# A diffusion backbone layer on one core: the down projection as seven quarter products instead of eight

## The chip, the cores and the metric

The kernel runs on one core of a Trainium2 chip. The metric is the device time of one execution in microseconds (us). The engines are named as in the profile: PE (matrix products; PEld are its weight loads), DVE (vector), ACT (scalar, activations), POOL, and SP, whose queue issues most of the DMAs. Lower is better.

## The reference, cut to what matters

One layer: a token mixer (spatial gating and gated linear attention, with a context prefix), then a channel mixer with a 3x3 depthwise convolution over the token grid, and a final norm. There are 512 tokens of 1024 channels and a hidden width of 2816, all in 32-bit floats. The change is in the second half of the channel mixer and in what follows it:

```python
def _conv_ffn(h, rows, w_up, conv_w, conv_b, w_down):
    a, val = _split(h @ w_up, (D_FF, D_FF))                  # 512 x 1024 @ 1024 x 5632
    ...                                                      # a: 3x3 depthwise convolution + bias
    return (gelu(a) * val) @ w_down                          # 512 x 2816 @ 2816 x 1024

x = x + g2x * _conv_ffn(hx2, ...)
return _rms_norm(x, final_norm_g)
```

## The kernel before, in words

Every large product is made of three products of fp32r operands: each 32-bit operand is split into a high half, which is a rounded copy, and a low half, which is the operand minus its high half, and high x high, high x low and low x high are accumulated in one PSUM bank. Splitting a tile is therefore one cast and one subtraction. For weights the cast is on ACT and the subtraction on DVE (`stream_split`, L186 and L187); for activations both are on DVE unless an engine is named (`split_act`, L273 and L274).

Weights come through one list, `specs`, in the order of their use, 512 KB an entry, loaded by SP's queue into four `raw` buffers (L174) and split into five `wh` and five `wl` buffers. `weights()` hands out the next entry and asks for the splits of two entries and the loads of three more.

The order of the instructions on each engine is set at compile time by a list scheduler: what stands earlier in the program has priority, and an instruction that is ready in its model may overtake one that isn't. Tiles come from pools of fixed size: `heap` (44 buffers of 2 KB a partition), `late` (27), and the PSUM pools `mm` and `gl` (four banks each). `in_order` adds edges that keep a group of instructions of an engine in program order.

In the up projection, 22 hidden tiles `f` of 128 channels are made. Each takes two products of 24 matmuls (L281), one for `a` and one for `val`, with the 512 tokens as columns. `conv_part` then copies `a` out of PSUM (ACT, L1183), starts the accumulator `cacc` with the middle tap (ACT, L1185), adds eight taps on DVE (L1191), applies Gelu (ACT, L1192) and multiplies by `val` (DVE, L1193). The 22 results stay in `heap` as `gact`, hidden channels on the partitions and tokens along the free side.

The down projection (from L1211 on) runs over two halves of the 1024 output columns, `hf`. A half has four PSUM banks, one for each tile of 128 tokens, and runs over the 22 hidden tiles; `down` (L1220 to L1225) issues the three matmuls of 512 columns. The first half also splits `gact` into `gs` (L273, L274); the second uses the same splits again. The last six hidden tiles, `TAIL`, are done token tile by token tile, so that the output of one tile can be finished while the next one is multiplied; the very last one is cut into 384 and 128 columns. `out_add` multiplies a bank by `g2` (L1232) and adds it to the residual `x1` (L1233), `out_step` also sums the squares (ACT, L1238), and `out_tok` makes the norm's factor (L1249 to L1251: DVE, ACT with Sqrt, DVE), scales both halves of the token tile (ACT L1253, DVE L1255) and stores them.

Of the kernel before, what the change touches and what calls it, by code (L numbers as in the profile page):

```python
# [33 lines left out]
def backbone_kernel(  # L34
# [212 lines left out]
    for d in range(2):  # L247
        raw = late([96, 512], s="w2r")
# [21 lines left out]
    def split_act(src, n=512, s="a", lo_pool=heap, hi_pool=heap, eng=None):  # L270
        hi = hi_pool([P, n], F32R, s=s + "h")
        lo = lo_pool([P, n], F32R, s=s + "l")
        (eng or V.tensor_copy)(hi, src)  # L273
        V.tensor_tensor(lo, src, hi.bitcast(F32), op=ALU.subtract)  # L274
        return hi, lo
# [311 lines left out]
    for k in range(KT):  # L587
        g = max(i for i in range(NG) if G0[i] <= k)
# [9 lines left out]
        n = 0  # L598
# [43 lines left out]
    for d in range(2):  # L642
        t_ = late([P, 4, P], s="pmask")
# [422 lines left out]
    for j in range(KT):  # L1066
        w = weights()
        ps = mm()
# [25 lines left out]
    for j in range(KT):  # L1094
        w = weights()
        ps = mm()
# [4 lines left out]
        w = weights()  # L1101
        ps = mm()
# [26 lines left out]
    for i in range(2):  # L1129
        ps = gl()  # L1130
# [44 lines left out]
    wide_tm(mg, wo_done, lambda: None)  # L1175


    gact = []

    def conv_part(f, pa, pv):  # L1180
        wcol = lambda tap: ccol[:, tap * FT + f:tap * FT + f + 1]
        a_ = heap([P, 8, GW], s="ca")
        A.copy(a_, pa)  # L1183
        acc = heap([P, 8, GW], s="cacc")
        A.activation(acc, pa, AF.Identity, bias=ccol[:, 198 + f:199 + f], scale=wcol(4))  # L1185
        for tap in (0, 1, 2, 3, 5, 6, 7, 8):
            dy, dx = tap // 3 - 1, tap % 3 - 1
            r0, r1 = max(0, -dy), 8 - max(0, dy)
            c0, c1 = max(0, -dx), GW - max(0, dx)
            o = acc[:, r0:r1, c0:c1]  # L1190
            V.scalar_tensor_tensor(o, a_[:, r0 + dy:r1 + dy, c0 + dx:c1 + dx], wcol(tap), o, op0=ALU.mult, op1=ALU.add)  # L1191
        A.activation(acc, acc, AF.Gelu)  # L1192
        V.tensor_tensor(acc, acc, pv.rearrange("p (r w) -> p r w", w=GW), op=ALU.mult)  # L1193
# [8 lines left out]
    conv_part(1, pss[2], pss[3])  # L1202
    for f in range(2, FT):
# [8 lines left out]
    for hf in range(2):  # L1212
        t_ = late([P, 512], s="fng")
        dma(t_, final_norm_g[hf * 512:(hf + 1) * 512].unsqueeze(0).to_broadcast([P, 512]))
        fng.append(t_)
    gs = []
    ss3 = const([P, 4, 3], "ss3")
    xg = []

    def down(ps, g, w, kk, t, c0, n, first, last):  # L1220
        gh, gl_ = g
        wh, wl = w
        for i, (a, b) in enumerate(((gh, wh), (gh, wl), (gl_, wh))):
            T.matmul(ps, a[:, t * P:(t + 1) * P], b[:, kk, c0:c0 + n], start=(first and i == 0),  # L1224
                     stop=(last and i == 2))  # L1225

    TAIL = 6

    def out_add(pv, hf, t, c0, n):
        tmp = late([P, n], s="yt")  # L1230
        xv = x1[t][hf][:, c0:c0 + n]
        V.tensor_tensor(tmp, pv, bc_g["g2", hf][:, c0:c0 + n], op=ALU.mult)  # L1232
        V.tensor_tensor(xv, xv, tmp, op=ALU.add)  # L1233
# [6 lines left out]
    def out_tok(t, part, before):  # L1240

        b_, r = small(1, "n3b"), small(1, "n3r")
        start = len(traced())
        part()
        if before > 1:
            V.reduce_sum(b_, ss3[:, t, :before], axis=AX.X)
            V.tensor_scalar(b_, b_, 1.0 / D, EPS, op0=ALU.mult, op1=ALU.add)
        else:
            V.tensor_scalar(b_, ss3[:, t, 0:1], 1.0 / D, EPS, op0=ALU.mult, op1=ALU.add)  # L1249
        A.activation(r, ss3[:, t, before:before + 1], AF.Sqrt, bias=b_, scale=1.0 / D)  # L1250
        V.reciprocal(r, r)  # L1251
        in_order(start, V.engine)
        A.mul(xg[t], xg[t], r)  # L1253
        adma(out[0, t * P:(t + 1) * P, 0:512], xg[t])
        V.scalar_tensor_tensor(x1[t][1], x1[t][1], r, fng[1], op0=ALU.mult, op1=ALU.mult)  # L1255
        dma(out[0, t * P:(t + 1) * P, 512:1024], x1[t][1])

    for hf in range(2):
        pss = [(mm if hf else gl)() for _ in range(4)]
        for kc_ in range((FT - TAIL) // 2):  # L1260
            w = weights()
            for kk in range(2):
                k = 2 * kc_ + kk
                if hf == 0:
                    gs.append(split_act(gact[k].rearrange("p r w -> p (r w)"), s="g"))
                for t in range(4):
                    down(pss[t], gs[k], w, kk, t, 0, 512, k == 0, hf == 1 and t == 3 and k == FT - TAIL - 1)
        wl3 = [weights() for _ in range(TAIL // 2)]
        if hf == 0:
            for k in range(FT - TAIL, FT):  # L1270
                gs.append(split_act(gact[k].rearrange("p r w -> p (r w)"), s="g", lo_pool=late))
        else:

            out_add(pss[3], 1, 3, 0, 512)
        for t in range(4):
            pieces = [(0, 384), (384, 128)] if hf and t == 3 else [(0, 512)]
            for i, (c0, n) in enumerate(pieces):
                ps = gl() if hf and t == 3 else pss[t]
                for k in range(FT - TAIL, FT):
                    down(ps[:, :n], gs[k], wl3[(k - FT + TAIL) // 2], k % 2, t, c0, n,  # L1280
                         hf == 1 and t == 3 and k == FT - TAIL, k == FT - 1)
                step = lambda: out_step(ps[:, :n], hf, t, c0, n, hf + i)
                if hf == 0 or i + 1 < len(pieces):
                    step()
                else:
                    out_tok(t, step, hf + i)
            if hf == 0:
                xg.append(late([P, 512], s="xg"))
                V.tensor_tensor(xg[t], x1[t][0], fng[0], op=ALU.mult)


# [28 lines left out]
```

## Time and profile before

| | us |
|---|---|
| median of three runs | 957.38 |
| lowest and highest | 956.77 and 957.75 |
| span of the profiled execution | 956.3 |
| PE busy | 935.2 |
| DVE busy | 654.4 |
| ACT busy | 351.0 |

For the profiled execution the page gives the span, from its first to its last instruction, and no device time of its own; the median lies 1.1 us above the span. The page cuts the span into 40 slices of 23.9 us, with the busy share of each engine in tenths. The up projection of the channel mixer ends at 828.5, the products of the down projection at 949.4. A line such as `L274 DVE TENSOR_TENSOR gl<-cacc,gh 128x512` reads: line of the kernel, engine, operation, tile written and tiles read, partitions x elements, and then the count, the busy time and the mean duration in ns. A line of the timeline begins with the start and the duration in us, and ends with the idle time before it and what ended it.

### The profile page before, as it was taken

To read this page: it belongs to the slowest core of one execution; us is meant where nothing else is said; L and a number is where in the kernel's file an instruction comes from. 1 tells how busy PE (TensorE), PEld (TensorE's weight loads), DVE (VectorE), ACT (ScalarE), POOL (GpSimd) and SP (SyncE) were. 2 spreads that over 40 slices of the span, in tenths; PEclk is the share of its full clock that TensorE was granted. 3 is DMA by queue.
4 is the path that set the end of the run, shared out by engine and by line. 5 is a ranking of instruction groups with operands and counts; after the bars stand their busy time and mean duration, and the time that the engine had idled before them with its cause. 6 is when DMAs were issued, how large, how long until landed. Compare 5 with 4: busy or idle time off the path is not lost.

```text
span 956.3 us, 12491 instructions
## 1 busy us (share of the span) xinstructions
PE 935.2 (98%) x4810; PEld 784.1 (82%) x4810; DVE 654.4 (68%) x1157; ACT 351.0 (37%) x593; POOL 13.4 (1%) x34
## 2 busy tenths in 40 slices
PE   6999999999999999999999999999999999999997
PEld 5677898988888888888878889988888888888886
DVE  5567768688699655597564357887777777893414
ACT  5146445566433222222222135433333333311313
POOL 3000000000000000000000000000000000000000
PEclk9999999999999999999999999999999999999999
DMA  9940412032137563683532443333333333232302
GB/s 274 342 126 24 113 43 61 29 111 67 38 118 220 173 205 85 215 270 104 158 91 88 148 122 111 103 96 88 110 89 105 93 89 110 69 114 84 110 1 88
DMA packets 147144, 111.95 MB, mean 117 GB/s; under 512 B 5849, under 2 KB 123941, under 8 KB 147085
## 3 DMA queue, kind: packets, MB, share of 16 engines
q1 hardware_dynamic: 145005, 109.72, 38.0%
q10 hardware_dynamic: 1728, 1.22, 0.4%
q8 instruction: 38, 0.62, 0.3%
q0 software_dynamic: 352, 0.22, 0.1%
q14 instruction: 21, 0.17, 0.1%
HBM read 109.04 MB, written 2.10 MB: 116 GB/s over the span
## 4 chain that ended last, share of the span: by engine, by line
PE 89%; DVE 5%; DMA 2%; ACT 2%; issue 1%; SPq 0%; ACTq 0%; DVEq 0%
PE mm L281 53%; PE gl L1224 7%; PE mm L1224 6%; PE mm L307 5%; PE gl L741 3%; PE mm L300 3%; PE mm L531 1%; PE mm L292 1%; PE gl L307 1%; PE mm L845 1%; DVE bc L709 1%; PE gl L531 1%; PE gl L772 1%; PE gl L1040 1%; PE gl L455 1%
## 5 line engine op out<-in xcount | busy, mean ns | idle before, releaser
L186 ACT CAST wh<-raw 128x1024 fp32r<-128x1024 f32 x140 | 147.3, 1053 | 368.1 <-PE mm L281 248.3
L187 DVE TENSOR_TENSOR wl<-raw,wh 128x1024 fp32r<-128x1024 f32 x140 | 170.6, 1220 | 126.4 <-ACT wh L186 126.0
L281 PE MATMUL mm<-h2h,wh 128*128 128x512 f32 (+1 forms) x352 | 133.5, 379 | 0.0
L281 PE MATMUL mm<-h2l,wh 128*128 128x512 f32 (+1 forms) x352 | 133.5, 379 | 0.0
L281 PE MATMUL mm<-h2h,wl 128*128 128x512 f32 (+1 forms) x352 | 133.5, 379 | 0.0
L1191 DVE SCALAR_TENSOR_TENSOR cacc<-ca,ccol,cacc 128x441 f32<-128x441 f32 (+2 forms) x176 | 121.8, 695 | 4.6 <-ACT cacc L1185 0.5
L281 PE MATMUL mm<-hxh,wh 128*128 128x512 f32 x296 | 116.5, 393 | 0.0
L281 PE MATMUL mm<-hxh,wl 128*128 128x512 f32 x296 | 115.7, 391 | 0.0
L281 PE MATMUL mm<-hxl,wh 128*128 128x512 f32 x296 | 115.4, 390 | 0.0
L281 PEld LDWEIGHTS mm<-h2h,wh 128*128 128x128 f32 x352 | 66.2, 188 | 12.6
L281 PEld LDWEIGHTS mm<-h2l,wh 128*128 128x128 f32 x352 | 66.2, 188 | 12.4
L281 PEld LDWEIGHTS mm<-h2h,wl 128*128 128x128 f32 x352 | 66.2, 188 | 12.4
L281 PEld LDWEIGHTS mm<-hxh,wl 128*128 128x128 f32 x296 | 55.6, 188 | 11.7 <-issue 0.2
L281 PEld LDWEIGHTS mm<-hxh,wh 128*128 128x128 f32 x296 | 55.6, 188 | 11.6 <-issue 0.5
L281 PEld LDWEIGHTS mm<-hxl,wh 128*128 128x128 f32 x296 | 55.6, 188 | 11.2 <-issue 0.2
L1008 DVE SCALAR_TENSOR_TENSOR acc<-wa,cs,acc 128x512 f32<-128x512 f32 x64 | 45.6, 744 | 4.8 <-DMA wa<-in_w_ada_dram 4.7
L1224 PE MATMUL gl<-wh,gl 128*128 128x512 f32 (+2 forms) x100 | 37.9, 379 | 0.0
L1224 PE MATMUL gl<-wl,gh 128*128 128x512 f32 (+2 forms) x100 | 37.9, 379 | 0.0
L1224 PE MATMUL gl<-wh,gh 128*128 128x512 f32 (+2 forms) x100 | 37.8, 378 | 0.0
L1192 ACT ACTIVATE cacc<-cacc 128x512 f32<-128x512 f32 x22 | 13.9, 632 | 60.5 <-DVE cacc L1191 60.5
L1224 PE MATMUL mm<-wh,gh 128*128 128x512 f32 x82 | 31.9, 389 | 0.0
L1224 PE MATMUL mm<-wl,gh 128*128 128x512 f32 x82 | 31.9, 389 | 0.0
(366 smaller groups left out, 1733.6 us busy)
## 6 DMA issues: line engine op xcount, KB each, us to landing
raw<-in_w_in_dram SPq DMA_DIRECT2D x54, 512.0 KB, 3.9
wa<-in_w_ada_dram SPq DMA_DIRECT2D x96, 256.0 KB, 4.9
raw<-in_ffn_w_up_dram SPq DMA_DIRECT2D x44, 512.0 KB, 3.8
raw<-in_ffn_w_down_dram SPq DMA_DIRECT2D x22, 512.0 KB, 3.6
raw<-in_w_br_a_dram SPq DMA_DIRECT2D x8, 512.0 KB, 4.5
raw<-in_w_br_b_dram SPq DMA_DIRECT2D x8, 512.0 KB, 4.3
raw<-in_w_o_dram SPq DMA_DIRECT2D x8, 512.0 KB, 3.6
xin<-in_x_dram SPq DMA_DIRECT2D x8, 256.0 KB, 3.2
```

The source lines that it names most:

```text
L186: A.copy(wh, raw)
L187: V.tensor_tensor(wl, raw, wh.bitcast(F32), op=ALU.subtract)
L281: T.matmul(ps, a[:, k, :], b[:, c0:c0 + n], start=(k == 0 and i == 0), stop=(k == KT - 1 and i == 2))
L292: T.matmul(ps, a[:, k, :], b[:, c0:c0 + n], start=(k == 0 and i == 0), stop=(k == KT - 1 and i == 2))
L300: T.matmul(ps, a[:, t * P:(t + 1) * P], b[:, k % 4, :], start=(k == 0 and i == 0), stop=(k == KT - 1 and i == 2))
L307: T.matmul(ps, a[:, t * P:(t + 1) * P], b[:, k % 2, :], start=(k == 0 and i == 0), stop=(k == KT - 1 and i == 2))
L531: T.matmul(fps[i], a, b, start=(k == 0 and z == 0), stop=(k == KT - 1 and z == 2))
L741: T.matmul(ps, p_, q_, start=(start and z == 0), stop=(stop and z == 2))
L1008: V.scalar_tensor_tensor(acc[j], w_, cs[:, k, 0:1], acc[j], op0=ALU.mult, op1=ALU.add)
L1191: V.scalar_tensor_tensor(o, a_[:, r0 + dy:r1 + dy, c0 + dx:c1 + dx], wcol(tap), o, op0=ALU.mult, op1=ALU.add)
L1192: A.activation(acc, acc, AF.Gelu)
L1224: T.matmul(ps, a[:, t * P:(t + 1) * P], b[:, kk, c0:c0 + n], start=(first and i == 0), stop=(last and i == 2))
```

## The change

The down projection is `G @ W` with `G` of 512 tokens x 2816 and `W` of 2816 x 1024. Both are cut into quarters: the tokens into two halves of 256, the output columns into two halves of 512, and the hidden tiles into the even ones (`e`, tile 2p of pair p) and the odd ones (`o`, tile 2p+1); there are eleven pairs. With A11, A21 the two token halves of `e`, A12, A22 those of `o`, B11, B12 the two column halves of the even rows of `W`, and B21, B22 those of the odd rows, the change makes (Winograd's form of Strassen's method):

```
S1 = A21 + A22   S2 = S1 - A11   S3 = A11 - A21   S4 = A12 - S2
T1 = B12 - B11   T2 = B22 - T1   T3 = B22 - B12   T4 = T2 - B21
P1 = A11 B11  P2 = A12 B21  P3 = S4 B22  P4 = A22 T4  P5 = S1 T1  P6 = S2 T2  P7 = S3 T3
C11 = P1 + P2       C12 = P1 + P6 + P5 + P3
C21 = P1 + P6 + P7 - P4       C22 = P1 + P6 + P7 + P5
```

Each of the seven products has 256 tokens, 512 columns and 1408 hidden channels. The first pass over the pairs makes P1, P5, P6 and P7 in eight banks. Then DVE and ACT combine them, and the second pass accumulates P2, P3 and P4 (its operand has the other sign) on top of three of the four. The sums over tokens, S1 to S4, are made on DVE in the up projection, after every second hidden tile (`token_sums`, four subtractions and additions of 256 columns). The sums over weights are made in `x_prep` (T1, T2 and T3, in the first pass) and `rb_prep` (T4). In all of them the high halves are now copied by ACT. Even rows come as `ra`, the right half of the odd rows as `b22`, a heap tile, and in the second pass the odd rows, whole, as `rb`. The program prepares two units ahead of the products (`LEAD`). The last three pairs of the second pass are done token tile by token tile, as the last six hidden tiles were.

The diff, cut to its core (the old down projection, which it takes out, and the entries of `ffn_w_down` in `specs` are left out; `out_tok` now takes the half that is finished last):

```diff
@@ up projection
+    def token_sums(p):
+        e, o = flat(gact[2 * p]), flat(gact[2 * p + 1])
+        s = late([P, 2, 256], s="s12")
+        if p % 2 == 0:
+            s4.append(late([P, 2, 256], s="s4"))
+        V.tensor_tensor(s[:, 0, :], e[:, 256:], o[:, 256:], op=ALU.add)
+        V.tensor_tensor(s[:, 1, :], s[:, 0, :], e[:, :256], op=ALU.subtract)
+        V.tensor_tensor(e[:, 256:], e[:, :256], e[:, 256:], op=ALU.subtract)
+        V.tensor_tensor(s4[-1][:, p % 2, :], o[:, :256], s[:, 1, :], op=ALU.subtract)
+        s12.append(s)
...
         gact.append(acc)
+        if f % 2:
+            token_sums(f // 2)
...
+    def d_raw(kind, p):
+        if kind == "b22":
+            t_ = heap([P, 512], s="b22")
+            dma(t_, tokens(2 * p + 1)[:, 512:])
+        else:
+            t_ = wp.tile([P, 2, 512], F32, tag="raw", name=nm("raw"), bufs=4)
+            dma(t_, tokens(2 * p + (kind == "rb")).rearrange("p (a c) -> p a c", c=512))
+        dq[kind, p] = t_
+    for p in range(NP):
+        dloads += [("ra", p), ("b22", p)]
+    dloads += [("rb", p) for p in range(NP)]
...
+    def split_into(wh, wl, raw):
+        A.copy(wh, raw)
+        V.tensor_tensor(wl, raw, wh.bitcast(F32), op=ALU.subtract)
+    def x_prep(p):
+        d_load(2 * p + 5)
+        ra, b22 = dq.pop(("ra", p)), dq["b22", p]
+        V.tensor_tensor(b22, b22, ra[:, 1, :], op=ALU.subtract)
+        V.tensor_tensor(ra[:, 1, :], ra[:, 1, :], ra[:, 0, :], op=ALU.subtract)
+        t2[p] = heap([P, 512], s="t2")
+        w = d_pair()
+        split_into(*w, ra)
+        e = split_act(flat(gact[2 * p]), s="e", eng=A.copy)
+        s = split_act(s12[p].rearrange("p a c -> p (a c)"), s="s", eng=A.copy)
+        V.tensor_tensor(t2[p], ra[:, 0, :], b22, op=ALU.add)
...
+    def t_prep(kind, ps_):
+        w = d_pair()
+        for j, p in enumerate(ps_):
+            src = dq.pop(("b22", p)) if kind == "t3" else t2[p]
+            split_into(w[0][:, j, :], w[1][:, j, :], src)
+        return w
+    def rb_prep(p):
+        d_load(2 * NP + p + 3)
+        rb = dq.pop(("rb", p))
+        V.tensor_tensor(t2[p], rb[:, 0, :], t2[p], op=ALU.subtract)
+        w = d_pair()
+        split_into(*w, rb)
+        o = split_act(flat(gact[2 * p + 1]), s="o", eng=A.copy)
...
+        if p % 2 == 0:
+            n = min(2, NP - p) * 256
+            s = split_act(s4[p // 2].rearrange("p a c -> p (a c)")[:, :n], n=n, s="s", eng=A.copy)
...
+    groups = [tuple(range(p, min(p + 2, NP))) for p in range(0, NP, 2)]
+    units = []
+    for g in groups:
+        units += [("x", (p,)) for p in g] + [("t3", g), ("t2", g)]
+    NX = len(units)
+    for g in groups[:-2]:
+        units += [("rb", (p,)) for p in g] + [("t4", g)]
+    units += [("rb", (p,)) for p in range(groups[-2][0], NP)] + [("t4", g) for g in groups[-2:]]
...
         pv = mm()
         prod_cm(pv, weights(), h2)
+        if f == FT - 1:
+            d_load(5)
         conv_part(f, pa, pv)
@@ down projection
+    def first_half(pv, hf, t):
+        out_step(pv, hf, t, 0, 512, 0)
+        xg[t] = late([P, 512], s="xg")
+        V.tensor_tensor(xg[t], x1[t][hf], fng[hf], op=ALU.mult)
...
+    for name, pool in (("p1", gl), ("p5", gl), ("p7", mm), ("p6", mm)):
+        bank[name] = [pool() for _ in range(2)]
+    LEAD = 2
...
+    for i in range(LEAD):
+        prep(i)
+    for i in range(NX - 3):
+        prep(i + LEAD)
+        steps_x(i)
+        if i == 8:
...
+    for i in (x_, t3_, t2_):
+        prep(i + LEAD)
+    steps_x(x_, "p1")
+    steps_x(t2_)
+    steps_x(t3_)
+    steps_x(x_, "p5")
+    for t in range(2):
+        p1s, p7s = heap([P, 512], s="p1s"), heap([P, 512], s="p7s")
+        A.copy(p1s, bank["p1"][t])
+        u = heap([P, 512], s="u2")
+        V.tensor_tensor(u, bank["p6"][t], p1s, op=ALU.add)
+        A.copy(p7s, bank["p7"][t])
+        V.tensor_tensor(bank["p5"][t], bank["p5"][t], u, op=ALU.add)
+        V.tensor_tensor(p7s, bank["p5"][t], p7s, op=ALU.add)
+        V.tensor_tensor(bank["p7"][t], bank["p7"][t], u, op=ALU.add)
+        c22.append(p7s)
...
+    prep(NX + 2)
+    steps_r(r0, "p1")
+    prep(NX + 3)
+    steps_r(r1, "p1")
+    steps_r(r0, "p5")
+    steps_r(r1, "p5")
+    for t in range(2):
+        first_half(c22[t], 1, 2 + t)
+    for i in range(NX + 2, MAIN):
+        prep(i + LEAD)
+        steps_r(i)
+    for i in range(MAIN + LEAD, len(units)):
+        prep(i)
+    out_add(bank["p7"][1], 0, 3, 0, 512)
...
+    for t in range(2):
+        for name, act, j in (("p1", "a12", 0), ("p5", "s4", 1)):
+            for n_, i in enumerate(rbs):
+                down(bank[name][t], ops[act, TAIL + n_], t, tw[i], j, False, True, again=True)
+            if j == 0:
+                first_half(bank[name][t], 0, t)
+        out_tok(t, 1, lambda: out_step(bank["p5"][t], 1, t, 0, 512, 1), 1)
+    for i, jj, p in t4s:
+        down(bank["p7"][0], ops["a22", p], 0, tw[i], jj, False, True, again=True)
+    out_tok(2, 0, lambda: out_step(bank["p7"][0], 0, 2, 0, 512, 1), 1)
+    for n_, (c0, n) in enumerate(((0, 384), (384, 128))):
+        ps = mm()
+        for i, jj, p in t4s:
+            down(ps[:, :n], ops["a22", p], 1, tw[i], jj, p == TAIL, p == NP - 1, c0, n)
...
```

More of the change, by code (lines that the diff above doesn't have):

```diff
@@ new lines, in backbone_kernel, with d_load, d_pair @@
+    for p in range(NP):
+        dloads += [("ra", p), ("b22", p)]
+    dloads += [("rb", p) for p in range(NP)]
+    dpos = [0]
+    def d_load(upto):
+        while dpos[0] < min(upto, len(dloads)):
+            d_raw(*dloads[dpos[0]])
+            dpos[0] += 1
+    def d_pair():
+        return tuple(wp.tile([P, 2, 512], F32R, tag=tag, name=nm(tag)) for tag in ("wh", "wl"))
+    def split_into(wh, wl, raw):
+        A.copy(wh, raw)
+        V.tensor_tensor(wl, raw, wh.bitcast(F32), op=ALU.subtract)
@@ new lines, in backbone_kernel @@
+    t2, ops = {}, {}
+    def x_prep(p):
[9 more added lines that the diff above has]
+        V.tensor_tensor(t2[p], ra[:, 0, :], b22, op=ALU.add)
+        ops["a11", p] = [z[:, :256] for z in e]
+        ops["s3", p] = [z[:, 256:] for z in e]
+        ops["s1", p] = [z[:, :256] for z in s]
+        ops["s2", p] = [z[:, 256:] for z in s]
+        return w
@@ new lines, in down @@
+    def down(ps, act, t, w, j, first, last, c0=0, n=512, again=False):
+        gh, gl_ = act
+        for i, (a, b) in enumerate(((gh, 0), (gh, 1), (gl_, 0))):
+            T.matmul(ps, a[:, t * P:(t + 1) * P], w[b][:, j, c0:c0 + n], start=(first and i == 0),
+                     stop=(last and i == 2), skip_group_check=again)
+    groups = [tuple(range(p, min(p + 2, NP))) for p in range(0, NP, 2)]
+    units = []
+    for g in groups:
+        units += [("x", (p,)) for p in g] + [("t3", g), ("t2", g)]
@@ L1203, in backbone_kernel, with prep @@
+    NX = len(units)
+    for g in groups[:-2]:
+        units += [("rb", (p,)) for p in g] + [("t4", g)]
+    units += [("rb", (p,)) for p in range(groups[-2][0], NP)] + [("t4", g) for g in groups[-2:]]
+    TAIL = groups[-2][0]
+    tw = {}
+    def prep(i):
+        if i < len(units):
+            kind, g = units[i]
+            tw[i] = x_prep(g[0]) if kind == "x" else rb_prep(g[0]) if kind == "rb" else t_prep(kind, g)
     for f in range(2, FT):
@@ L1207, in backbone_kernel @@
         prod_cm(pv, weights(), h2)
+        if f == FT - 1:
+            d_load(5)
         conv_part(f, pa, pv)
     fng = []
[L1212 to L1216, printed above, removed]
-    ss3 = const([P, 4, 3], "ss3")
[L1218 to L1227, printed above, removed]
+    ss3 = const([P, 4, 3], "ss3")
+    xg = [None] * 4
     def out_add(pv, hf, t, c0, n):
@@ L1238, in out_step, with out_tok @@
         A.activation(tmp, xv, AF.Square, accum_out=ss3[:, t, part:part + 1])
[L1240 removed]
+    def first_half(pv, hf, t):
+        out_step(pv, hf, t, 0, 512, 0)
+        xg[t] = late([P, 512], s="xg")
+        V.tensor_tensor(xg[t], x1[t][hf], fng[hf], op=ALU.mult)
+    def out_tok(t, hf, part, before):
         b_, r = small(1, "n3b"), small(1, "n3r")
@@ L1252, in out_tok @@
         in_order(start, V.engine)
+        o = 1 - hf
         A.mul(xg[t], xg[t], r)
[L1254 to L1271, printed above, removed]
-        else:
[L1274 to L1289, printed above, removed]
@@ new lines, in out_tok, with steps_x @@
+        adma(out[0, t * P:(t + 1) * P, o * 512:(o + 1) * 512], xg[t])
+        V.scalar_tensor_tensor(x1[t][hf], x1[t][hf], r, fng[hf], op0=ALU.mult, op1=ALU.mult)
+        dma(out[0, t * P:(t + 1) * P, hf * 512:(hf + 1) * 512], x1[t][hf])
+    bank = {}
+    for name, pool in (("p1", gl), ("p5", gl), ("p7", mm), ("p6", mm)):
+        bank[name] = [pool() for _ in range(2)]
+    LEAD = 2
+    def steps_x(i, only=None):
+        kind, g = units[i]
+        for name, act, j in ((("p1", "a11", 0), ("p5", "s1", 1)) if kind == "x" else
+                             ((("p7", "s3", None),) if kind == "t3" else (("p6", "s2", None),))):
+            if only and name != only:
+                continue
+            for jj, p in enumerate(g):
+                for t in range(2):
+                    down(bank[name][t], ops[act, p], t, tw[i], jj if j is None else j, p == 0, p == NP - 1)
@@ new lines, in steps_r @@
+    def steps_r(i, only=None):
+        kind, g = units[i]
+        for name, act, j in ((("p1", "a12", 0), ("p5", "s4", 1)) if kind == "rb" else (("p7", "a22", None),)):
+            if only and name != only:
+                continue
+            for jj, p in enumerate(g):
+                for t in range(2):
+                    down(bank[name][t], ops[act, p], t, tw[i], jj if j is None else j, False, True, again=True)
+    for i in range(LEAD):
[4 more added lines that the diff above has]
+        if i == 8:
+            for hf in range(2):
+                t_ = late([P, 512], s="fng")
+                dma(t_, final_norm_g[hf * 512:(hf + 1) * 512].unsqueeze(0).to_broadcast([P, 512]))
+                fng.append(t_)
@@ new lines, in backbone_kernel @@
+    MAIN = len(units) - 5
+    r0, r1 = NX, NX + 1
+    prep(NX + 2)
[4 more added lines that the diff above has]
+    steps_r(r1, "p5")
+    for t in range(2):
+        first_half(c22[t], 1, 2 + t)
[5 more added lines that the diff above has]
+    out_add(bank["p7"][1], 0, 3, 0, 512)
+    rbs = range(MAIN, MAIN + 3)
+    t4s = [(MAIN + 3, 0, TAIL), (MAIN + 3, 1, TAIL + 1), (MAIN + 4, 0, TAIL + 2)]
@@ new lines, in backbone_kernel @@
+    for t in range(2):
+        for name, act, j in (("p1", "a12", 0), ("p5", "s4", 1)):
[7 more added lines that the diff above has]
+    out_tok(2, 0, lambda: out_step(bank["p7"][0], 0, 2, 0, 512, 1), 1)
```

22 lines of the change are left out of this document (18 added, 4 removed).

## The prediction

> **What bounds the kernel now.** I read the page first, then the chain of waits over the last 170 us, then the busy table by stretches.
>
> ```profile
> PE 935.2 (98%) x4810; PEld 784.1 (82%) x4810; DVE 654.4 (68%) x1157; ACT 351.0 (37%) x593; POOL 13.4 (1%) x34
> DVE  5567768688699655597564357887777777893414
> ...
> GB/s 274 342 126 24 113 43 61 29 111 67 38 118 220 173 205 85 215 270 104 158 91 88 148 122 111 103 96 88 110 89 105 93 89 110 69 114 84 110 1 88
> ```
> ```profile
> 828.68 59.84 PE gl L1224 x264
> 888.52 55.76 PE mm L1224 x246
> 944.28 5.12 PE gl L1224 x36
> ...
> 951.03 0.75 DVE x L1255
> ```
> ```profile
> 817.00:828.00 11.00, 11.00 (x50) 9.13 (x49) 8.69 (x14) 3.90 (x5) 0.00 (x0) 1.00 0.30 103
> 828.00:850.00 22.00, 22.00 (x99) 18.22 (x98) 21.76 (x38) 4.75 (x5) 0.00 (x0) 1.00 0.29 96
> 850.00:888.00 38.00, 38.00 (x169) 31.45 (x169) 20.16 (x30) 8.84 (x13) 0.00 (x0) 1.00 0.22 74
> 888.00:925.00 37.00, 37.00 (x165) 30.65 (x164) 11.80 (x12) 8.60 (x10) 0.00 (x0) 1.00 0.22 72
> 925.00:950.00 25.00, 24.38 (x122) 20.93 (x120) 9.95 (x22) 7.13 (x15) 0.00 (x0) 1.00 0.17 63
> ```
> The first fence: PE is busy 98% of the span, DVE 68%, but its slices sink to 3, 4 and 1 at the end. The second is the end of the chain: the down projection is 546 matmuls (264, 246, 36) without a break, from 828.5 to 949.4, then a short tail through DVE to 951.78; its stores end at the span's end, 956.3, 4.5 later. The third (columns: PE, weight loads, DVE, ACT, POOL, clock, DMA share, GB/s) says the same by stretches: PE full; DVE full just behind the seam (21.76 of 22), then 20.16 of 38 and 11.80 of 37. So PE sets the pace, and in its second half DVE is two thirds idle. The change lives on that idle time.
>
> The page gives no device time for the profiled execution; I take the 1.1 us by which the runs' median (957.4) exceeds the span (956.3) as what lies around it. A difference of 0.2%, 1.9 us, is about what a measurement here can tell.
>
> **PE's side.** One matmul of 512 columns costs 59.84 / 264 = 0.2267 us. Before, 528 full products were needed, 18 of them cut into pieces of 384 and 128. After: seven products x 2 token tiles x 11 pairs x 3 terms = 462, nine of them cut. 66 x 0.2267 = 15.0 us go. A cut pair costs 5.12 / 18 = 0.284, or 0.058 more than one whole; nine cuts fewer give 0.5. PE alone would save 15.5 us: span 940.8.
>
> **DVE's side: its price per instruction.**
>
> ```profile
> 814.42 5.10 DVE L1191 SCALAR_TENSOR_TENSOR cacc<-ca,ccol,cacc 128x441 f32<-128x441 f32 x7
> ...
> 822.01 0.69 DVE L1193 TENSOR_TENSOR cacc<-cacc,mm 128x512 f32<-128x512 f32 x1 [0.76 <-ACT cacc L1192]
> 824.14 1.23 DVE L187 TENSOR_TENSOR wl<-raw,wh 128x1024 fp32r<-128x1024 f32 x1 [1.45 <-ACT wh L186]
> 825.28 0.42 DVE L273 CAST gh<-cacc 128x512 fp32r<-128x512 f32 x1
> 825.62 0.67 DVE L1191 SCALAR_TENSOR_TENSOR cacc<-ca,ccol,cacc 128x441 f32<-128x441 f32 x1
> 826.21 0.69 DVE L274 TENSOR_TENSOR gl<-cacc,gh 128x512 fp32r<-128x512 f32 x1
> 826.81 0.68 DVE L1191 SCALAR_TENSOR_TENSOR cacc<-ca,ccol,cacc 128x448 f32<-128x448 f32 x1
> ...
> 834.22 1.22 DVE L187 TENSOR_TENSOR wl<-raw,wh 128x1024 fp32r<-128x1024 f32 x1
> 835.36 0.68 DVE L1193 TENSOR_TENSOR cacc<-cacc,mm 128x512 f32<-128x512 f32 x1
> ...
> 932.08 0.69 DVE L1232 TENSOR_TENSOR yt<-mm,g 128x512 f32<-128x512 f32 x1 [8.57 <-PE mm L1224]
> ...
> 932.80 0.69 DVE L1233 TENSOR_TENSOR x<-x,yt 128x512 f32<-128x512 f32 x1
> ```
> A two-operand instruction of 512 columns takes 0.69, but where the next doesn't need its result, starts lie 0.595 apart (825.62, 826.21, 826.81). One of 1024 columns holds the engine 1.14 (834.22 to 835.36). Where the next needs the result, 512 columns cost 0.72 (932.08 to 932.80). I take 0.595 for operand preparation, whose neighbours are independent (the high halves move to ACT), and 0.72 for chains.
>
> *First pass, per pair:* two subtractions, the sum `t2`, and the low halves of `e`, `s`, T3 and T2: seven of 512; and the low half of `ra`, one of 1024. 7 x 0.595 + 1.14 = 5.31 us, against 24 x 0.2267 = 5.44 of PE. Eleven pairs: 58.4.
> *Second pass, per pair:* `t2`, the low halves of `o` and T4, that of `rb`: 3 x 0.595 + 1.14 = 2.93, against 18 x 0.2267 = 4.08. Eleven pairs 32.2, and `s4` (five of 512, one half as long) 3.3: 35.5.
> *Between:* eight PSUM combinations at 0.69, 5.5; two `first_half` of three chained operations, 6 x 0.72 = 4.3.
>
> ```profile
> L1255 DVE SCALAR_TENSOR_TENSOR x<-x,n3r,fng 128x512 f32<-128x512 f32 x4 | 3.0, 752 | 0.1
> ...
> L1251 DVE RECIPROCAL n3r<-n3r 128x1 f32<-128x1 f32 x4 | 0.7, 164 | 5.0 <-ACT n3r L1250 5.0
> ...
> L1232 DVE TENSOR_TENSOR yt<-gl,g 128x384 f32<-128x384 f32 x1 | 0.5, 549 | 0.0
> L1249 DVE TENSOR_SCALAR n3b<-ss 128x1 f32<-128x1 f32 x3 | 0.4, 147 | 0.0
> L1232 DVE TENSOR_TENSOR yt<-gl,g 128x128 f32<-128x128 f32 x1 | 0.3, 292 | 0.6 <-PE gl L1224 0.6
> ```
> *Tail:* `out_add` 1.4; two `first_half` 4.3; three `out_tok` of 2 x 0.72 + 0.15 + 0.16 + 0.75 = 2.5, 7.5; the piece of 384, 1.1; the last piece 2 x 0.29 + 0.3 + 0.16 + 0.75 = 1.8: 16.1.
> *Token sums:* 256 columns lie between the 292 and 549 ns rows, about 0.42, so at most 1.7 a pair. DVE idles 0.76 and 1.45 per hidden tile of the up projection (L1193, L187), 4.4 a pair: ten of eleven groups of sums are covered, and PE doesn't wait for DVE there. Without that cover they would cost 17 us. The last group, 1.5, falls behind the seam.
>
> **When can DVE start?**
>
> ```profile
> 813.13 0.58 ACT L1183 COPY ca<-mm 128x512 f32<-128x512 f32 x1
> ...
> 823.05 1.05 ACT L186 CAST wh<-raw 128x1024 fp32r<-128x1024 f32 x1 [1.08 <-PE mm L281]
> ...
> 824.48 0.78 ACT L1185 ACTIVATE cacc<-mm,ccol 128x512 f32<-128x512 f32 x1
> ```
> ```profile
> raw<-in_ffn_w_down_dram SPq DMA_DIRECT2D x22, 512.0 KB, 3.6
> ```
> Here I chose. The weight splits run ahead of their place in the program (L186 at 823.05), but the first cast of `g`, whose input is the first conv tile of the up projection, starts at 825.28, right behind the last tile's `cacc` (824.48 + 0.78). I read this as: heap tiles are handed out in program order. The first `b22` stands between the last two conv tiles, so it is loaded no earlier than `ca` of tile 20 (813.13); 3.6 to land gives 817.5. The L187 splits of down weights that DVE now does earlier are gone, and their time with them. At 817.5 conv tile 20 still owes three of the seven taps of L1191 in that row, the eighth and L1193: 5 x 0.6 = 3.0; tile 21 owes nine: 5.4.
>
> Sum from 817.5: 3.0 + 5.4 + 1.5 + 58.4 + 5.5 + 35.5 + 4.3 + 16.1 = 129.7, to 947.2. PE from 828.5 has 120.9 - 15.5 = 105.4, to 933.9. So DVE becomes the bound, and PE idles some 13 us: at the end of the first pass, where the last low halves are late; while DVE combines; behind `first_half`, ahead of the fourth `rb`; and in the tail, where DVE's 16.1 exceed PE's 12.7 (54 products and nine cuts). The waits of ACT in the last chain (the Square and Sqrt between L1233 and L1251) add 0.8, the stores 4.5: 952.5. Bounds of what I can't see: nothing, or 6 us of DVE idle. I take 2.0, near the low end: DVE left no hole behind the seam before; 1.0 for the first operands, which pass DVE, DVE, ACT (1.05) and DVE in turn, and 1.0 for an uncovered wait for ACT at L1251 (5.0 over four there). Span 954.5, time **955.6 us**.
>
> DMA: `b22` is read twice, so 768 KB a pair instead of 512 KB a chunk, 145 GB/s at 5.4 us a pair; loads stand two pairs ahead on SP, whose queue holds nothing else, and the page's slices reach 342. I cost it at nothing; late, it would be DVE that waits at `ra`. The two `fng` loads move behind unit 8 on the same queue, long ahead of their first use: nothing. ACT takes the high halves: 1.05 + 4 x 0.58 = 3.4 of the 5.3 us of a first-pass pair, hidden as long as it runs ahead. The second bank of `p6` is free only when L1193 of tile 21 has read the last `val` product (835.36 before); PE wants it after 36 products, at 836.7: a hole of PE's at worst, and PE has slack.
>
> **Rivals.**
> *DVE keeps its full duration (slower).* If neighbours do wait for each other (a subtraction into what the one before reads, a low half right behind ACT's copy), each 512 costs 0.69 and each 1024 1.22: 115 x 0.095 + 22 x 0.08 + 0.8 for the conv = 13.5, giving 969.1. It ends above before by more than 0.2% from 3.7 us of loss on, a mean start distance above 0.625. For: the pairs of cast and subtraction, chained, lay further apart. Against: the three starts above, in the same crowded place.
> The Trainium skill, "VectorE: DVE Perf Modes", section "The DRAIN you can't avoid", says the next operation doesn't start until the pipe is empty; read as full durations that is this rival's 969. The same section lets an instruction that isn't held start earlier, and the trace's 0.595 agrees with that.
>
> *The preparation hides under the up projection (faster).* If heap tiles are not dealt in order, the 4.4 us a pair of idle DVE, less the sums' 1.7, take enough that PE stays the bound: 940.8, plus 5.5 - 2.7 for the combinations (PE has twelve products meanwhile), plus 16.1 - 12.7 for DVE's lag in the tail, plus 1.1: 948.1. Against it: the 825.28 start.
>
> *PE's clock falls in the new holes.*
>
> ```profile
> 20.00:30.00 10.00, 8.71 (x86) 6.37 (x87) 5.66 (x13) 3.30 (x6) 0.00 (x0) 0.83 1.17 299
> ```
> ```profile
> 21.29 0.80 PE L531 MATMUL gl<-hxh,qkh 128*128 128x512 f32 x1 [1.89 <-ACT xT L424]
> ```
> A hole of 1.89 us stands in a stretch whose granted clock is 0.83, 1.7 us of PE lost in 10. Two such holes, at the combinations and behind `first_half`, cost 3.4 if DVE's lead doesn't cover them: 959.0. Against: PE has slack against DVE.
> The Trainium skill, "TensorE: Matmul & The Clock Gate", section "HAM oscillation — how this bites in real kernels", puts the drop to half rate at an idle window above about 3.4 us; by that only the longer hole would count, one drop, 957.3.
>
> **How the numbers follow.** Forecast 0.58 (953 to 959.5, as its loss runs from nothing to 6; half of it below 955.5, a little above 959.3: 0.28 faster, 0.28 same, 0.02 slower); full durations 0.16 (959.5 to 969), slower; hidden preparation 0.14 (947 to 953), faster; the clock 0.12 (957.5 to 962), 0.04 same and 0.08 slower. Faster 0.42, same 0.32, slower 0.26. The range 950 to 964 leaves out about half of each outer case, under 0.2.
>
> **What would show it.** PE x4735; DVE about 1281 instructions (66 fewer, 190 more); PE busy tenths below 9 behind the seam, with DVE as releaser; DVE at 9 from about 820 to 947. Right: starts of preparation 0.6 apart, and the first one just behind `ca` of tile 20. Wrong: DVE idle for more than 6 us in there, preparation before 813, or a first pass that PE fills without a hole.

## The result, and the profile after

After the change the median is 951.48 us (950.66 to 952.52, four runs), against 957.35 before: a ratio of 0.9938, with a 95% interval of 0.9924 to 0.9952. It is faster by 5.9 us. The forecast was 955.6 in a range of 950 to 964, and the profiled execution has a span of 949.0 where 954.5 was forecast. So the sign and the mechanism have to be tested, and 5.5 us of the span explained.

The page after: engines, then the slices of 23.7 us and PE's granted clock.

```profile
span 949.0 us, 12570 instructions
...
PE 918.8 (97%) x4735; PEld 768.9 (81%) x4735; DVE 720.4 (76%) x1281; ACT 389.4 (41%) x669; POOL 13.4 (1%) x34
...
PE   6999999999999999999999999999999999999995
...
DVE  5567768688599645597674447798888888899997
...
PEclk9999999999999999999999999999999999999998
```

The counts are those that were announced (4735 and 1281). The tail of DVE's row, `...3414` before, is now `...9997`, while PE's falls to 5 in the last slice. The same stretches as before (PE, weight loads, DVE, ACT, POOL, clock, DMA share, GB/s) show it better:

```profile
817.00:828.00 11.00, 11.00 (x51) 9.09 (x50) 10.47 (x16) 6.28 (x10) 0.00 (x0) 1.00 0.07 24
828.00:850.00 22.00, 19.83 (x87) 15.77 (x86) 22.00 (x38) 10.18 (x17) 0.00 (x0) 1.00 0.54 168
850.00:888.00 38.00, 38.00 (x166) 30.60 (x165) 37.78 (x55) 23.44 (x37) 0.00 (x0) 1.00 0.39 125
888.00:925.00 37.00, 36.25 (x159) 29.35 (x158) 37.00 (x55) 24.84 (x41) 0.00 (x0) 1.00 0.31 101
925.00:950.00 25.00, 12.93 (x64) 11.00 (x62) 18.50 (x39) 10.20 (x25) 0.00 (x0) 0.83 0.23 84
```

DVE was busy 20.16 of 38 and 11.80 of 37 us in the third and fourth stretch; now it is 37.78 and 37.00. PE is full in only one of the stretches behind the seam. (The clock of 0.83 in the last row belongs to the time behind PE's last product; up to 937.9 it is 1.00.) What DVE itself waited for between 814 and 945, and PE between 820 and 950 (total, times, longest):

```profile
DVE n3r L1355 <- ACT n3r L1354: 0.9, 2, 0.7
DVE wl L1245 <- ACT wh L1244: 0.5, 1, 0.5
```
```profile
PE gl L1295 <- ACT wh L1244: 2.0, 1, 2.0
PE gl L1295 <- ACT p1s L1410: 0.8, 2, 0.5
```

DVE has 1.4 us of waits in 130, and the 0.9 lies in the last chain. PE's 2.0 is one hole at 843.95. It names ACT. What ACT waited for in turn is read from the times:

```profile
842.07 0.70 DVE L1254 TENSOR_TENSOR raw<-raw 128x512 f32<-128x512 f32 x1
```
```profile
842.85 1.04 ACT L1244 CAST wh<-raw 128x1024 fp32r<-128x1024 f32 x1 [3.14 <-PE gl L1295]
```
```profile
843.95 0.74 PE L1295 MATMUL gl<-wh,eh 128*128 128x512 f32 x2 [2.02 <-ACT wh L1244]
```

ACT's row names PE, but the hole before 843.95 had begun at 841.93, 0.92 ahead of the cast. DVE's subtraction in the same tile ended at 842.77, 0.08 ahead of it. So the hole goes back to DVE.

From the timeline, the hand-over at the seam, DVE in the crowded first pass, and the end:

```profile
827.72 0.39 PE L1295 MATMUL gl<-wh,eh 128*128 128x512 f32 x1
...
937.65 0.28 PE L1295 MATMUL mm<-wh,ol 128*128 128x128 f32 x1
```
```profile
847.48 0.69 DVE L1253 TENSOR_TENSOR b<-b,raw 128x512 f32<-128x512 f32 x1
848.08 0.69 DVE L271 TENSOR_TENSOR el<-cacc,eh 128x512 fp32r<-128x512 f32 x1
...
929.80 0.71 DVE L1331 TENSOR_TENSOR yt<-mm,g 128x512 f32<-128x512 f32 x1
...
943.81 0.75 DVE L1360 SCALAR_TENSOR_TENSOR x<-x,n3r,fng 128x512 f32<-128x512 f32 x1
```

Starts of 512-column preparation lie 0.60 apart. PE issues its last product at 937.65, and DVE works until 944.56, 6.6 us beyond PE's end (2.4 before). The stores take the last 4.4.

### The profile page after: what moved, and what is told of

The parts are those of the page before. It is cut to its first block, busy times and chain, and to the rows that moved or that the text cites. A ratio compares the mean times of both kernels' runs of the same rounds, so it can differ in the third digit from the quotient of the medians.

```text
span 949.0 us, 12570 instructions
## 1 busy us (share of the span) xinstructions
PE 918.8 (97%) x4735; PEld 768.9 (81%) x4735; DVE 720.4 (76%) x1281; ACT 389.4 (41%) x669; POOL 13.4 (1%) x34
## 5 line engine op out<-in xcount | busy, mean ns | idle before, releaser
L278 PE MATMUL mm<-obh,wh 128*128 128x512 f32 x64 | 24.9, 390 | 0.0
L278 PE MATMUL mm<-obl,wh 128*128 128x512 f32 x64 | 24.9, 389 | 0.0
L278 PE MATMUL mm<-ah,wh 128*128 128x512 f32 x64 | 24.9, 389 | 0.0
```

Source lines behind the costliest of these rows:

```text
L278: T.matmul(ps, a[:, k, :], b[:, c0:c0 + n], start=(k == 0 and i == 0), stop=(k == KT - 1 and i == 2))
```

## The experiments

The theory: from some 815 on DVE is the bound without a pause, so that an instruction more or less on DVE moves the end by its start distance, and PE has slack. The first rival: what sets the end is the order of the work (the combinations between the passes, the chain at the end), and the amount on DVE doesn't matter; 951.5 for all.

PE's work ahead of the seam is the same in all these kernels, but in the profiled executions the first product of the down projection starts anywhere from 826.6 to 831.4. So beside the medians and ratios the table gives the stretch from that start to the end of the span, which is free of this; it is that of one execution for each kernel. Each ratio is to before on the same chip.

| run | what differs from after | median | ratio (interval) | seam to end | to after |
|---|---|---|---|---|---|
| before | | 957.35 | 1 | 127.8 | +6.5 |
| after | | 951.48 | 0.9938 (0.9924 to 0.9952) | 121.3 | 0 |
| e1 | 10 DVE instructions fewer | 946.79 | 0.9881 (0.9864 to 0.9898) | 116.3 | -5.0 |
| e2 | 18 matmuls more | 952.62 | 0.9945 (0.9930 to 0.9960) | 122.0 | +0.7 |
| e3 | 11 DVE instructions more | 958.49 | 1.0007 (0.9997 to 1.0016) | 128.2 | +6.9 |
| e4 | 35 DVE instructions fewer | 943.77 | 0.9850 (0.9834 to 0.9867) | 114.0 | -7.3 |
| e5 | before, with the token sums | 957.24 | 0.9994 (0.9985 to 1.0004) | | |
| e6 | sums called behind the seam | 951.64 | 0.9931 (0.9915 to 0.9947) | 121.7 | +0.4 |
| e10 | sums held behind the seam | 966.89 | 1.0089 (1.0063 to 1.0115) | 134.9 | +13.6 |
| e7 | first loads one tile earlier | 949.70 | 0.9911 (0.9891 to 0.9931) | 120.1 | -1.2 |
| e8 | first loads two tiles earlier | 949.96 | 0.9925 (0.9907 to 0.9943) | 119.9 | -1.4 |
| e9 | as e7, first unit ahead too | 949.03 | 0.9908 (0.9886 to 0.9929) | 118.9 | -2.4 |
| e11 | `t2` on POOL | 958.60 | 1.0012 (1.0003 to 1.0022) | 128.9 | +7.6 |
| e12 | one pair done plainly, loads as in e7 | 945.96 | 0.9884 (0.9867 to 0.9900) | 116.2 | -5.1 |

**Less and more work on each engine (e1 to e4).** One kernel makes the low half of `e` for the first pair alone and uses it for all (`split_shared` copies the high half and keeps the low half of its first call):

```diff
-        e = split_act(flat(gact[2 * p]), s="e", eng=A.copy)
+        e = split_shared(flat(gact[2 * p]), "e", s="e")
```

> Seven products, with ten instructions fewer on DVE: the low half of e is made for the first pair alone and all eleven pairs use that tile (so P1 and P7 lack the right low terms); PE's and ACT's work is unchanged. Theory (DVE sets the pace from 815 us on, every 512-column operand costs 0.60 us of its time): 10 x 0.60 = 6.0 us less than the changed kernel's 951.5, 945.5; not under 944, because PE then runs its first pass without a hole. Rival (PE sets the pace, its holes come from waits that have nothing to do with DVE's load): 951.5, no change.

The second adds products to PE and nothing to DVE:

```diff
         steps_r(i)
+        kind, g = units[i]
+        if kind == "t4" and g[0] < 6:
+            for t in range(2):
+                down(bank["p6"][t], ops["a22", g[0]], t, tw[i], 0, True, True)
```

> The changed kernel with 18 products of 512 columns more, in the second pass, into the two banks of P6, which nobody reads any more: 18 x 0.2267 = 4.1 us of PE. Theory (DVE is the bound; in the tail PE ends 6.7 us ahead of DVE's last instruction where before it was 2.4, so PE has some 4.3 us to give): 951.5, at most 1 us more. Rival (PE is the bound): 955.6.

The third adds one addition per pair of the second pass to DVE:

```diff
+        more = heap([P, 512], s="more")
+        V.tensor_tensor(more, rb[:, 0, :], rb[:, 1, :], op=ALU.add)
         w = d_pair()
```

> The changed kernel with one more DVE instruction of 512 columns for each pair of the second pass, whose result nobody reads: 11 x 0.60 = 6.6 us of DVE. Theory (DVE is the bound): 958.1. Rival (DVE's load is covered by PE): 951.5, at most 1 us more.

The fourth shares the low halves of `e`, `s`, `o` and `s4`:

> As the first, for the low halves of e, s, o and s4: ten, ten, ten and five instructions fewer on DVE (the products use the low halves of the first pair throughout), 21 us of DVE. Theory: DVE no longer is the bound, PE is; 105.4 us of PE from 827.7 end at 933.1, some 2 us of holes at the combinations, then a tail of DVE of 3 to 5 us, the stores 4.4: span 943 to 944.5, time 944.3 to 946. So the 15.5 us that PE saves mostly arrive where DVE is relieved. Rival (the holes are PE's own): 951.5.

Eleven instructions more, 6.6 us at 0.60, cost 6.9 behind the seam and 6.6 by the ratios. Ten fewer, 6.0, brought 5.0 (5.5 by the ratios); the median, 946.79, misses the 945.5 that was expected, and DVE's waits in that trace are 0.8 longer than after. Eighteen matmuls, 4.1 us of PE's time, cost 0.7 (1.1 by the medians), and their interval overlaps that of after. So DVE's amount sets the end, and the rival falls. With 35 fewer, 21 us, only 7.3 come: PE is the bound again, and 943.77 lies 0.5 below the range expected for that. Its page's busy line, and PE by stretches:

```profile
PE 920.6 (98%) x4735; PEld 771.3 (82%) x4735; DVE 700.6 (74%) x1246; ACT 390.2 (41%) x669; POOL 13.4 (1%) x34
```
```profile
828.00:850.00 22.00, 22.00 (x97) 17.82 (x96) 21.96 (x37) 12.95 (x22) 0.00 (x0) 1.00 0.54 180
850.00:888.00 38.00, 38.00 (x170) 31.45 (x169) 32.57 (x47) 23.36 (x38) 0.00 (x0) 1.00 0.42 136
888.00:925.00 37.00, 37.00 (x165) 30.65 (x164) 30.59 (x43) 23.39 (x39) 0.00 (x0) 1.00 0.25 82
```

PE is full in all three, and no wait of PE is listed. Its products run from 828.90 to 934.6, 105.7 us. That is what seven products cost when nothing else limits them, and 943.8 is the time of this kernel with PE as its bound.

**Where the token sums lie (e5, e6, e10).** The first puts the sums alone into the kernel before, with the old down projection; their results are not used.

> One part of the change alone: the kernel before, with its old down projection, and the four token operations after every second hidden tile, whose results nobody uses. 44 instructions, 1.35 us a group, 14.9 us of DVE in all. Theory (the up projection leaves DVE 4.4 us idle for each pair of tiles, and PE doesn't wait for it): no change, 957.4, at most 0.5 more. Rival (the sums delay the convolution's tiles and so PE's banks): up to 15 us more.

957.24 against 958.09: 44 instructions more on DVE, no cost that can be measured, and no wait of PE in the up projection. The next was to take their cover away by calling them in the preparation of their pair:

```diff
-        if f % 2:
-            token_sums(f // 2)
...
         d_load(2 * p + 5)
+        token_sums(p)
```

> One part undone: the seven products, but each pair's token sums are made in the first pass, just ahead of its operands. Ten groups of 1.35 us move from the up projection's idle DVE time into the stretch that DVE bounds. Theory: 13.5 us more than the changed kernel, 965, slower than before. Rival (PE covers them): 951.5.

The expectation failed, because the edit didn't do what it said. The line's own view (count, duration min/median/max in ns, first and last start):

```profile
L1184 DVE TENSOR_TENSOR s<-cacc,cacc x11: 421/425/425, 624.9 to 879.5; 128x256 f32<-128x256 f32 x11
```

Groups that stand behind the seam in the program ran from 624.9 on: the list scheduler put all but the last of them back into the gaps of the up projection, and 951.64 is the time of after once more. In the next kernel they are held behind the weight subtractions of their pair:

```diff
+        start = len(traced())
         V.tensor_tensor(b22, b22, ra[:, 1, :], op=ALU.subtract)
         V.tensor_tensor(ra[:, 1, :], ra[:, 1, :], ra[:, 0, :], op=ALU.subtract)
+        token_sums(p)
+        in_order(start, V.engine)
```

> All token sums are made behind the seam: each pair's group of four (0.42 us each, some 1.35 us from start to start) is called behind the two weight subtractions of its pair and held there on DVE, so that the scheduler can't pull it back into the gaps of the up projection as it did in the run before. Nothing of the computation changes. Theory (DVE is the bound from 815 on without idle time, and the up projection hid ten groups): ten groups more on the path, 10 x 1.35 = 13.5 us, 965 (between 961 and 967). Rival (DVE is not what sets the end): within 2 us of 951.5.

```profile
L1184 DVE TENSOR_TENSOR s<-cacc,cacc x11: 421/425/439, 820.8 to 896.2; 128x256 f32<-128x256 f32 x11
```

Now all eleven lie behind 820, the first of them still ahead of this execution's seam (831.0) but in the stretch that DVE bounds, and the end comes 13.6 us later (14.5 by the ratios), for 13.5 expected. The gaps of the up projection are worth that much to this change. The four sums of a pair start 0.34 apart where they follow one another, so the 17 us of the prediction, from whole durations of 0.42, was too dear.

**When DVE starts (e7, e8, e9).** One line decides where the first weight loads stand in the program:

```diff
-        if f == FT - 1:
+        if f == FT - 2:
             d_load(5)
```

> The changed kernel with its first five loads placed one hidden tile earlier in the program, ahead of conv tile 20's tiles instead of tile 21's; the DVE order then has the first preparations inside conv tile 19. Theory (heap tiles are dealt in program order, that is what holds the first preparations back, and DVE is the bound): the first preparation 10.9 us earlier, at 804, some 3 us of idle DVE ahead of 815 filled: 948.5 to 950. Rival (the start doesn't matter, or loads collide with the up projection's): 951.5 or more.

> The first weight loads of the down projection are called three hidden tiles before the last instead of with the last one. Nothing of the computation changes. Theory (heap tiles are dealt in program order, so the first b22 lands earlier and the first preparation with it, in gaps of the up projection): DVE starts its work some 3 to 5 us earlier, 947 to 949.7. Rival (the start of the preparation doesn't matter, or the earlier tile takes a buffer that the up projection needs): 951.5 or more.

In e8 the line reads `FT - 3`: two hidden tiles earlier than after. The third, e9, is e7's edit, and also calls the preparation of the first unit ahead of the last conv tile:

> As the one before, and the first pair is also prepared ahead of the last conv tile in the program, so that its t2, e and s tiles are dealt first. Theory: the same gain and up to 1 us more, as DVE has more work that it may take into its gaps: 947.5 to 950. Rival: the last conv tile comes later, and with it the bank that the second P6 needs: PE waits at the seam, 951 to 953.

The first preparation starts at 814.93 after, at 804.26 in e7 and at 793.73 in e8, a hidden tile earlier each time. The medians lie below that of after, though the intervals overlap with its own, and behind the seam the end moves by only 1.2, 1.4 and 2.4 us; e8's 949.96 misses its range, 947 to 949.7, as the second step earlier brought almost nothing more. What an earlier start can use is DVE's idle time ahead of the seam, and there is little: in the 37.7 us ahead of it DVE was busy 32.33 us after, and 33.12, 33.37 and 34.34 in these three. The 0.8, 1.0 and 2.0 that they filled are each 0.4 below what the end gained.

**Another engine for a part of DVE's work (e11).** The sum `t2` and its subtraction go to POOL:

```diff
-        V.tensor_tensor(t2[p], ra[:, 0, :], b22, op=ALU.add)
+        G.tensor_tensor(t2[p], ra[:, 0, :], b22, op=ALU.add)
...
-        V.tensor_tensor(t2[p], rb[:, 0, :], t2[p], op=ALU.subtract)
+        G.tensor_tensor(t2[p], rb[:, 0, :], t2[p], op=ALU.subtract)
```

> The sum t2 of the first pass and its subtraction in the second, 22 instructions of 512 columns, go from DVE to POOL. Nothing of the computation changes. Taken from DVE alone: 22 x 0.60 = 13 us; with DVE no longer the bound PE is, as in the run with the low halves shared: 943.8 to 946. Rival (a POOL instruction on SBUF operands holds up DVE while it runs, or POOL is so slow that t2 comes late): the gain is eaten, 951.5 or more, and DVE's starts beside a POOL instruction lie more than 0.6 apart.

The theory's hope fell and its rival held: 958.6. DVE has 22 instructions fewer, and is busy 722.3 us against 720.4. Two places of the timeline show why. In the first POOL starts ahead of DVE's instruction, in the second into a dense row of them:

```profile
836.45 1.27 POOL L1260 TENSOR_TENSOR t<-raw,b 128x512 f32<-128x512 f32 x1 [9.62 <-ACT sh L270]
...
864.08 8.01 POOL L1260 TENSOR_TENSOR t<-raw,b 128x512 f32<-128x512 f32 x1 [4.40 <-ACT wh L1244]
```
```profile
836.39 0.67 DVE L1203 TENSOR_TENSOR cacc<-cacc,mm 128x512 f32<-128x512 f32 x1
836.99 1.28 DVE L1254 TENSOR_TENSOR raw<-raw 128x512 f32<-128x512 f32 x1
...
863.77 0.68 DVE L271 TENSOR_TENSOR sl<-s,sh 128x512 fp32r<-128x512 f32 x1
864.37 1.21 DVE L1245 TENSOR_TENSOR wl<-raw,wh 128x1024 fp32r<-128x1024 f32 x1
...
870.26 0.68 DVE L1245 TENSOR_TENSOR wl<-t,wh 128x512 fp32r<-128x512 f32 x1
872.77 0.69 DVE L1245 TENSOR_TENSOR wl<-t,wh 128x512 fp32r<-128x512 f32 x1 [1.84 <-ACT wh L1244]
```

At 836.45 POOL takes 1.27 us, and DVE's instruction beside it takes 1.28 instead of 0.68: it ends 0.55 behind POOL's end (837.72, 838.27). At 864.08 POOL's instruction takes 8.01 us, while DVE goes on at 0.60; it ends at 872.09, 1.15 behind the end of DVE's row (870.94). ACT's cast and then DVE wait for it, 1.84. So once it is DVE that waits, and once POOL, whose operand then comes late; in all, DVE's waits are 7.5 us here, for 1.4 after. The Trainium skill, "SBUF — State Buffer", section "Who interferes with whom", says that a VectorE instruction with two inputs in SBUF contends with a GpSimd instruction that reads SBUF for a port that is an exclusive lock, and that the order of issue decides who blocks. The first place agrees with it. In the second, nine DVE instructions that start behind POOL's listed start went ahead of it, which the order of issue alone doesn't explain.

**A version to keep (e12).** Per pair the seven products cost DVE 8.3 us, where eight plain ones with their casts on ACT cost 3.5 (2 x 1.14 + 2 x 0.60), and save PE 1.4. So the last pair goes plainly, at the head of the second pass, and the load stands as in e7:

```diff
-    groups = [tuple(range(p, min(p + 2, NP))) for p in range(0, NP, 2)]
+    groups = [(0, 1), (2, 3), (4, 5), (6,), (7, 8), (9,)]
...
+    units += [("plain", "ra"), ("plain", "rb")]
...
+    def plain_prep(kind):
+        d_load(2 * NQ + (kind == "rb") + 3)
+        w = d_pair()
+        split_into(*w, dq.pop((kind, NQ)))
+        z = split_act(flat(gact[2 * NQ + (kind == "rb")]), s="e", eng=A.copy)
...
+    steps_plain(r0, "p1")
     prep(NX + 3)
...
+    steps_plain(r1, "p1")
+    for name in ("p5", "p7", "p6"):
+        steps_plain(r0, name)
+        steps_plain(r1, name)
     for t in range(2):
+        V.tensor_tensor(c22[t], bank["p6"][t], c22[t], op=ALU.add)
         first_half(c22[t], 1, 2 + t)
```

> A version to keep, made from what the runs before showed: ten pairs by the seven products, and the last pair (hidden tiles 20 and 21) plainly, at the head of the second pass, its eight products straight onto the four results (the one for C22 through the idle banks of P6); the first weight loads are called one hidden tile earlier. Nothing of the computation is left out. Theory (DVE sets the end until PE binds again): DVE loses one pair's preparation and its share of S4 (8.3 + 0.4 us) and the group of token sums behind the seam (1.4), and gains two low halves of 1024 columns, two of 512 and two additions (4.7): 5.4 us less; the earlier load gives 2 more. PE gets 6 matmuls more, 1.4 us, over the 943.8 at which it bound with the low halves shared: 945 to 947. Rival (the order of work behind the combinations, not the amount of DVE's, sets the end): no better than the run with the earlier load alone, 949 to 951.5.

```profile
PE 921.8 (98%) x4741; PEld 772.0 (82%) x4741; DVE 714.8 (76%) x1270; ACT 387.9 (41%) x664; POOL 13.4 (1%) x34
...
PE   6999999999999999999999999999999999999996
...
DVE  5567759688699845598564446798888888999997
```

945.96, within what was expected, and faster than both kernels. Against e7, which differs from it by the plain pair and the grouping that goes with it, the end behind the seam comes 3.9 us earlier (2.6 by the ratios), for 5.4 expected. PE has no wait listed, and DVE is at 9 beside it up to the last slice: the two engines are nearly in balance. Whether a second plain pair would bring more was not tried.

## Why the prediction was right, and where its numbers were off

**PE's side** was right. 75 matmuls went; seven products alone, forecast at 120.9 - 15.5 = 105.4, measure 105.7 in e4.

**DVE becomes the bound:** right, and shown by e1 and e3 against e2.

**DVE's sum** of 129.7 stands against 944.56 - 814.93 = 129.6, but in part by luck. The sum measured holds 1.4 of waits and, since DVE began earlier, one tap of conv tile 20 more, 0.6. Taken alike, 129.7 + 0.6 stands against 128.2: prices were 2.1 too dear. The prepared operands cost what was said. The chains did not cost 0.72 or 0.69 a link:

```profile
893.41 0.70 DVE L1414 TENSOR_TENSOR gl<-gl,u 128x512 f32<-128x512 f32 x1
894.01 0.69 DVE L1416 TENSOR_TENSOR mm<-mm,u 128x512 f32<-128x512 f32 x1
894.60 0.69 DVE L1415 TENSOR_TENSOR p7s<-gl,p7s 128x512 f32<-128x512 f32 x1
```

The combinations start 0.60 apart, because the schedule puts other work between an instruction and the one that needs it. The same in the tail: 929.80 to 944.56 is 14.8 with its waits, for 16.1 + 0.8.

**The start of DVE's work** is the step that failed in its cause. The first preparation came just behind `ca` of tile 20, as announced, 2.6 us ahead of the forecast's 817.5 (0.8 of it because this whole execution stands 0.8 earlier at the seam). But the prediction said that `b22` is loaded no earlier than `ca` of tile 20. The rows say otherwise; the second and third are from the view of that tile:

```profile
811.60 0.59 ACT L1193 COPY ca<-mm 128x512 f32<-128x512 f32 x1 [2.32 <-PE mm L278]
```
```profile
L1224 SPq DMA_DIRECT2D b<-in_ffn_w_down_dram x7: 327/423/968, 803.2 to 845.6; - x7
...
DMA to landing us min/median/max: 2.6/3.2/3.8
```
```profile
811.18 0.42 DVE L1187 TENSOR_TENSOR s<-cacc,s 128x256 f32<-128x256 f32 x1
812.90 2.12 DVE L1201 SCALAR_TENSOR_TENSOR cacc<-ca,ccol,cacc 128x441 f32<-128x441 f32 x3 [1.30 <-ACT cacc L1195]
814.93 0.69 DVE L1253 TENSOR_TENSOR b<-b,raw 128x512 f32<-128x512 f32 x1
```

The load was issued at 803.2 and landed by 807.0, before `ca`; the first `raw`, its other operand, had been issued at 787.25. The preparation was ready and stood still, because in DVE's order it comes behind three taps of tile 20, and DVE idled 1.30 us for those. So it is the order made at compile time that sets the start. Why the scheduler put it there (what its model held for the load) was not tried. That the place of the call in the program moves the start by a hidden tile is shown by e7 and e8.

**The loss of 2.0** was not there: 0.5 of DVE's waits lie outside the tail, where 0.8 had been priced and 0.9 came. I had put it at the low end, and the low end was right: with work of two passes in reach, the scheduler found something for DVE at the combinations and at the first operands.

In sum: 2.6 for the start, 2.9 for prices and loss (129.7 + 0.8 + 2.0 against 129.6), and 0.1 for the stores make 5.5 to 5.6, the miss in the span. What lies around the span is 1.66 (950.66 and 949.0), not 1.1, which gives 0.6 back; and the median lies 0.8 above the profiled run.

**PE's idle time** lay elsewhere. The holes that were placed at the end of the first pass, at the combinations and at the fourth `rb` came to 0.8 together, with one of 2.0 in the first pass at 843.95. Most of PE's slack is the 6.6 us at the end, so the announced sign, busy tenths of PE below 9 behind the seam, shows in the last slice alone. Why the holes closed up was not tried; that the scheduler took products in another order as operands came is a guess. From the seam to its last product PE took 110.2 us, 4.5 more than the 105.7 of e4; the waits listed are 2.8 of these. Part of the rest hides under "busy": from 850 to 888 PE is listed as busy throughout, but starts 166 products, where e4 starts 170.

**The token sums** are covered, as said (e5); the price without cover was 13.6, not 17 (e10). The loads had been put at nothing, and no wait of DVE behind 814 names a DMA.

**The rivals.** Full durations on DVE: not seen, 0.60 in the most crowded place. A hidden preparation: no. The measured time lies in the band that this rival had, 947 to 953, and not in the forecast's own, from 953 on; that is luck for the rival, as DVE and not PE is the bound. e4 shows the time with PE as the bound, 943.8 where the rival had 948.1, and e12 comes near it with 946.0. PE's clock: not in the changed kernel; the granted clock is 1.00 in the stretch that holds the hole of 2.02 and in the one with the combinations. But it did fall in two of the experiments that gave PE longer holes, first e10, then e11 (in the second row of each, the 0.50 is the granted clock):

```profile
908.00 0.50 PE L1296 MATMUL gl<-wh,oh 128*128 128x512 f32 x1 [3.14 <-ACT p1s L1411]
```
```profile
910.00:912.00 2.00, 2.00 (x6) 1.61 (x6) 2.00 (x5) 1.38 (x3) 0.00 (x0) 0.50 0.44 94
```
```profile
883.90 0.50 PE L1295 MATMUL gl<-wl,eh 128*128 128x512 f32 x1 [2.32 <-DVE wl L1245]
```
```profile
886.00:888.00 2.00, 2.00 (x6) 1.61 (x5) 2.00 (x5) 0.00 (x0) 0.65 (x1) 0.50 0.38 154
```

About 1 us behind the hole the clock went to half, for some 3.4 us with the neighbouring stretches, so that PE lost 1.7 each time; DVE remained busy throughout both rows. The Trainium skill, "TensorE: Matmul & The Clock Gate", section "HAM oscillation — how this bites in real kernels", has the clock drop at an idle window above some 3.4 us. Here it fell behind holes of 3.14 and 2.32 and not behind one of 2.02, so a shorter hole was enough than that page has.

## What to carry to other kernels

A method that takes products from PE pays in vector work. Count that work per unit at its start distance (here 0.60 us for 512 columns, 8.3 us a pair where the plain form has 3.5) against what PE saves (1.4 us a pair), and see how long the other engine's idle time lasts: here DVE's idle time paid for ten pairs, and the eleventh was better done plainly. With the two engines near balance, moving one unit back brought 3.9 us here, where starting DVE earlier brought 1.2 to 2.4. Before reading an experiment on a scheduled kernel, look in its trace for whether the edit took effect: an order that is made at compile time can undo it, as in e6.

## What was not expected of the hardware

A POOL instruction on SBUF operands isn't free beside DVE: at its shortest 1.27 us for 512 columns, against a dense row of DVE instructions up to 8.0, and where it came first DVE's instruction grew from 0.68 to 1.28. Moving 13 us of DVE's work there made the kernel 7 us slower than after. And PE's granted clock fell to 0.50 for some 3.4 us behind holes of 3.14 us (e10) and 2.32 us (e11).
